# Modulation vectors stored to DRAM after one transpose on TensorE, in rows of 512 bytes

## The chip, the cores and the metric

The kernel runs on one core of one Trainium2 chip. The metric is the device time of an execution in microseconds (us); the median of three runs stands for a kernel.

## The reference

The kernel computes a two-part network on 512 tokens of width 1024. The first part is a block that a condition vector `c` modulates: six vectors of 1024 come from it, and four of them are used late, after the mixer. What matters of it, cut down:

```python
mod_x = silu(c) @ w_mod + b_mod                       # 6 x 1024 values
sh1, sc1, gt1, sh2, sc2, gt2 = split(mod_x, 6)
px = modulate(rms_norm(x, norm1), sh1, sc1) @ w_in    # modulate(h, s, g) = h * (1 + g) + s
...
x = x + gt1 * (concatenate([na_x, hg_x]) @ w_out)
x = x + gt2 * peer_ffn(modulate(rms_norm(x, norm2), sh2, sc2), ...)
```

`na_x` is an attention over neighbours and a context (queries, keys and values are the first 1536 columns of `w_in`), `hg_x` a gated linear recurrence (its forget gates `f` are columns 2048 to 3071). A second part of two layers follows, which the change does not touch.

## The kernel before, in words

Matrix products run on TensorE (PE) with each float32 operand split into a high and a low part, three products for one. A weight tile `w` is loaded by SP into a ring of four (`WBUFS`), ACT writes its high part `wh` and DVE the low part `wl`, two buffers each. Everything is written in the order of generators that `weave` interleaves by their declared costs; each engine then runs its own instructions in order. PSUM has eight banks of 128 x 512, handed out in turn.

The stretch of the change lies in `mixer`. There `weave(self.project_na(first), self.late_mods())` interleaves two things:

- `project_na` projects queries, keys and values. Its last part is the V projection (512 columns in four weight chunks of two k-steps, 18 products each), after which ACT copies four banks into `F`, PE turns them into seven banks of V rows (line 585 and the `ident,F` rows of line 122), and DVE copies two and then seven banks to `V` (lines 577 and 590).
- `late_mods` makes the vectors `gt1`, `sh2`, `sc2` and `gt2`, 1024 values each, held as 128 partitions x 8. Each of the 32 steps (`mod_chunk`) loads 128 rows of `w_mod` transposed (512 KB, through the same ring `w`), multiplies them on DVE by the condition row with a running sum (line 332), and adds the bias (line 333).

The vectors are also needed as rows, the same 1024 values in every partition. `keep_rows` therefore stores each of them (for `sc2` the gain `a2`, line 361) to the DRAM tile `Rd`, through POOL's queue, and `rows_of` later loads a row into all partitions. A vector lies across partitions, so every element of the store is a piece of 4 bytes:

```python
self.nc.gpsimd.dma_start(self.Rd[n].rearrange("(k p) -> p k", p=128), vec)
```

It is called four times, each time as soon as its vector is complete. After that, `lower_bounds` computes a small table `lbm` and stores it to the DRAM tile `Ld` by ACT's queue (line 446, 128 x 2 pieces of 32 bytes). Then `weave(self.project_f(), self.na_tiles(na))` interleaves the projection of the forget gates (`f`, line 611, weights of 256 columns) with 32 tiles of attention: scores (lines 887 and 890), bias added by DVE (892, the bias loaded by SP, 882), maximum (894), exponential on ACT (896), transposes of `P` (903) and products with V.

Of the kernel before, what the change touches and what calls it, by code (L numbers as in the profile page):

```python
# [7 lines left out]
F32 = mybir.dt.float32  # L8
# [4 lines left out]
OP = mybir.AluOpType  # L13
# [3 lines left out]
D = 1024  # L17
S = 512
C = 256
KC = D // 128  # L20
# [31 lines left out]
def run(gen):  # L52
    while True:
        try:
            next(gen)
        except StopIteration as e:
            return e.value


def steps(gen, n):  # L60
    for _ in range(n):
        yield next(gen)


def weave(*gens):

    at = [[0.0, i, g] for i, g in enumerate(gens)]
    while at:
        cur = min(at, key=lambda x: (x[0], x[1]))
        try:  # L70
            cur[0] += next(cur[2])
        except StopIteration:
            at.remove(cur)
# [18 lines left out]
class Net:  # L92
# [262 lines left out]
        self.nc.vector.tensor_tensor(out=m[:, n], in0=b[:, :4].rearrange("p (j i) -> p j i", j=2),  # L355
                                     in1=self.bm[:, n:n + KC + 1:KC].unsqueeze(2).to_broadcast([128, 2, 2]), op=OP.add)

    def gain_of(self, vec, scale, j, name):

        o = self.g.tile([128, KC], F32, name=name)  # L360
        self.nc.vector.scalar_tensor_tensor(o, scale[:, :, j], 1.0, self.gains[:, vec], op0=OP.add, op1=OP.mult)
        return o

    def keep_rows(self, n, vec):

        self.nc.gpsimd.dma_start(self.Rd[n].rearrange("(k p) -> p k", p=128), vec)

    def rows_of(self, n, name, pool):

# [5 lines left out]
    def mixer(self):  # L375
        y = self.pool("y")
        self.Y = y.tile([128, 4, 512], F32, name="Y")
        self.open_stream()
        pj = self.pool("pj")
        hh = pj.tile([128, KC, C + S], FR, name="hh")  # L380
        hl = pj.tile([128, KC, C + S], FR, name="hl")
        self.project_setup(pj, hh, hl)
        first = self.proj(self.p['win'], 0, 512, [self.xs])
        for n in self.mix_norm(hh, hl):
            if n % 2:
                next(first)
        m = self.pool("mixf", "right")
        self.F = m.tile([128, 2, 6, 512], F32, name="F")
        self.mixn = m = self.pool("mixn", "right")
        self.q2 = m.tile([128, 8, S], FR, name="q2")  # L390
        self.k2 = m.tile([128, 8, S + C], FR, name="k2")
        self.ql = m.tile([128, 4, S], FR, name="ql")
        self.V = m.tile([128, 9, 512], F32, name="V")
        weave(self.project_na(first), self.late_mods())
        with self.after(self.last_v):
            self.lower_bounds()
        self.shut("mp")
        na = self.pool("na", "right")
        weave(self.project_f(), self.na_tiles(na))
        self.shut("na")  # L400
        self.shut("mixn")
        m = self.pool("mixi", "right")
        self.I = m.tile([128, 6, 512], F32, name="I")
        self.G = m.tile([128, 4, 512], F32, name="G")
        self.hq = m.tile([128, 4, S], F32, name="hq")
        self.load_bounds()
        q = self.project_q()
        for _ in range(2):
            next(q)
        with self.after(self.last_exp):  # L410
            self.gates()
        run(q)
        self.shut("lbt")
        run(self.project_g())
        hg = self.pool("hg", "right")
        kv = []
        values = self.project_i()
        next(values)
        with self.after(self.log_table(self.last_sig)):
            weave(values, self.hg_keys_decayed(hg, kv))  # L420
        self.shut("pj")
        self.shut("st")
        self.hg_chunks(hg, kv)
# [38 lines left out]
                nc.vector.tensor_tensor(out=f, in0=f, in1=self.lb[:, d:d + 1].to_broadcast([128, 3, 512]), op=OP.add)  # L462

    def late_mods(self):
        self.Rd = self.tc.dram_tile([4, D], F32, name="Rd")
        for j, name in ((2, "gt1"), (3, "sh2"), (4, "sc2"), (5, "gt2")):
            t = self.g.tile([128, KC, 1], F32, name=name)
            setattr(self, name, t)
            for k in range(KC):
                self.mod_chunk(j, t[:, k], k)  # L470
                yield 3.0
            if j in (2, 3, 5):
                self.keep_rows((2, 3, 5).index(j) + (j > 2), t[:, :, 0])
            if j == 4:
                self.a2 = self.gain_of(1, t, 0, "a2")
                self.keep_rows(1, self.a2)

    def mix_norm(self, hh, hl):

# [548 lines left out]
    def peer(self):  # L1028
        nc, p = self.nc, self.p
        hh, hl = self.h2  # L1030
        mv = ([hh[:, k] for k in range(KC)], [hl[:, k] for k in range(KC)])
        first = self.proj_first(self.ws, mv, lambda i: self.normed_half(i, [(hh, hl, self.a2)], 1e-6, self.sh2[:, :, 0]))
        self.finish = None
        for name in ("wo", "st", "hca", "y", "pn"):
            self.shut(name)
        mk = self.pool("mk")
        self.mk = mk.tile([128, 2, 2, C], F32, name="mk")
        self.mv = mk.tile([128, 2, 2, C], F32, name="mv")
        self.open_stream()
        self.Wd = self.tc.dram_tile([TD // WT, 128, 128, WT], F32, name="Wd")  # L1040
        self.Ad = self.tc.dram_tile([AHEAD, 128, TD], F32, name="Ad")
        pg = self.pool("pg", "right")
        self.rows_natural(pg)
        sc = self.queries(mv, first)
        pq = self.pool("pq", "right")
        ac = self.pool("ac")
        pa = self.pool("pa")
        dense = tuple([x[:, T0:] for x in part] for part in mv)
        ahead = self.ahead(pa, dense)
        self.chosen = None  # L1050
        gather = self.gathered(pg, ac)
        with self.tc.manual_schedule(engines={mybir.EngineType.PE}):
            weave(self.route(pq, pg, sc), steps(ahead, AHEAD - REST), self.until_routed(gather))
        self.shut("pq")
        self.shut("psc")
        run(ahead)
        self.shut("pa")
        pm = self.pool("pm", "right")
        ar = self.pool("ar")
        for i in range(GROUP - WLATE):  # L1060
            self.spread_rows(pm, 0, i)
        rows = self.rows_of(3, "gt2r", ar)
        banks = [[self.bank() for _ in range(2)] for _ in range(3)]
        ops = {}
        held = []
        left = self.gather_left
        done = 0
        for e in range(128 + OPS_LAG):
            if e < 128:
                ops[e] = self.operands(pm, e, dense)  # L1070
            want = left * min(e + 1, 120) // 120
            for _ in range(done, want):
                next(gather, None)
            done = max(done, want)
            if e >= OPS_LAG:
                x = e - OPS_LAG
                if x < 128 - TAIL:
                    self.products(banks, range(3), [(x, ops.pop(x))])
                else:
                    held.append((x, ops.pop(x)))  # L1080
        run(gather)
        for t in range(3):
            self.products(banks, [t], held)
        for name in ("pm", "pg", "h2"):
            self.shut(name)
        pt = self.xp = self.pool("pt", "right")
        nf = pt.tile([128, D], F32, name="nf")
        nc.scalar.dma_start(nf, self.rowb(p['normf'], D))
        self.ss = ss = self.sp.tile([128, 4, 2], F32, name="ssx")
        self.xh = {}  # L1090
        self.ws = [self.first_weights(p['awin'], 2304, q) for q in range(2)]
        for t in range(4):
            sq = self.sp.tile([128, 2], F32, name="ssp")
            for h in range(2):
                b = banks[t - 1][h] if t else self.accg[:, h * 512:(h + 1) * 512]
                hs = slice(h * 512, (h + 1) * 512)
                y = pt.tile([128, 512], F32, name="y2", bufs=2)
                nc.vector.tensor_tensor(out=y, in0=b, in1=rows[:, hs], op=OP.mult)
                nc.vector.tensor_tensor(out=self.X[:, t, hs], in0=self.X[:, t, hs], in1=y, op=OP.add)
                self.square_sum(self.X[:, t, hs], sq[:, h:h + 1], pt.tile([128, 512], F32, name="sqx", bufs=2))  # L1100
            r = self.rstd(sq, 1e-6)
            for h in range(2):
                hs = slice(h * 512, (h + 1) * 512)
                nc.vector.scalar_tensor_tensor(self.X[:, t, hs], self.X[:, t, hs], r, nf[:, hs], op0=OP.mult, op1=OP.mult)
                self.square_sum(self.X[:, t, hs], ss[:, t, h:h + 1], pt.tile([128, 512], F32, name="sqx", bufs=2))
            self.unit(t, 1e-5, 4)
        self.shut("ar")
        self.shut("ac")
# [751 lines left out]
```

## Time and profile before

| | |
|---|---|
| median of three runs | 3135.5 us (3133.11 to 3138.17) |
| profiled execution, its time | 3140.31 us |
| profiled execution, its span | 3138.5 us |
| mean granted clock of TensorE | 0.969 of full speed |
| busy: PE, DVE, ACT, POOL | 94%, 60%, 41%, 14% of the span |
| chain that ended last: PE, DVE, DMA | 59%, 18%, 8% of the span |

The profile is of one execution; the times it gives are set against that execution's own time, which is 4.8 us above the median. Busy shares are means over the whole span. What a stretch waits for is read from its own rows: the timeline of an engine gives the idle time before an instruction and what ended it, the table by stretch gives each engine's busy time, the clock that PE was granted (1.00 is full speed), the share of time in which the 16 DMA engines worked, and what they moved.

### The profile page before, as it was taken

What the parts mean: (1) busy time and instruction counts of PE and PEld (TensorE: products, weight loads), DVE (VectorE), ACT (ScalarE), POOL (GpSimd) and SP (SyncE); (2) the same over time, 40 slices, a digit from 0 to 9 for tenths busy, and PEclk for the clock granted to TensorE, in tenths of its full rate; (3) what the DMA queues carried; (4) which work ended last, traced back from release to release, by engine and by line L of the source; (5) the groups of instructions that cost most, each with busy time, mean ns of one, the idle gap of its engine ahead of it and who ended that gap; (6) DMA issues with size and microseconds to landing.
All of it is one profiled execution on the core that took longest, in us unless ns stands there. A gap on an engine that the chain in (4) does not pass through costs nothing.

```text
span 3138.5 us, 42272 instructions
## 1 busy us (share of the span) xinstructions
PE 2946.8 (94%) x16009; PEld 2528.4 (81%) x16009; DVE 1890.9 (60%) x3640; ACT 1271.9 (41%) x2275; POOL 442.8 (14%) x402
## 2 busy tenths in 40 slices
PE   7879898999999999988898888899999999999998
PEld 5668797889899999967677777778888887788887
DVE  5644477639999966678788886544433245543323
ACT  4223464344366677633333323433323234433222
POOL 2200000100211210144454441000000000000000
PEclk9989999999999999999999999999999999999999
DMA  6832202334676776899999996222333222133332
GB/s 244 188 83 72 88 8 68 111 118 135 228 235 220 250 248 238 273 360 372 351 379 370 358 373 220 65 75 89 101 95 100 95 88 68 48 88 100 94 101 81
DMA packets 259148, 539.89 MB, mean 172 GB/s; under 512 B 21632, under 2 KB 136576, under 8 KB 254592
## 3 DMA queue, kind: packets, MB, share of 16 engines
q1 hardware_dynamic: 198368, 347.92, 34.9%
q0 software_dynamic: 36992, 134.25, 11.9%
q10 hardware_dynamic: 23584, 55.03, 4.7%
q8 instruction: 125, 2.05, 0.3%
q14 instruction: 79, 0.65, 0.1%
HBM read 487.02 MB, written 50.09 MB: 171 GB/s over the span
## 4 chain that ended last, share of the span: by engine, by line
PE 59%; DVE 18%; DMA 8%; issue 2%; ACT 1%; SPq 1%; POOL 0%; ACTq 0%; DVEq 0%; POOLq 0%
PE bank L122 57%; DMA act<-Ad 4%; DMA w<-in_V_dram 2%; DVE wl L1351 2%; DVE vl L135 2%; DVE gr L1163 2%; DVE accg L1168 2%; DMA gr<-in_Un_dram,iu 1%; DVE sl L135 1%; PE bank L611 1%; DVE act L1390 1%; PE bank L1499 1%; DVE tmp L1241 1%; DVE eq L1280 1%; DVE eq L1282 1%
## 5 line engine op out<-in xcount | busy, mean ns | idle before, releaser
L122 PE MATMUL bank<-hh,wl 128*128 128x512 f32 (+2 forms) x2304 | 840.5, 365 | 36.3 <-DVE wl L1351 18.4
L122 PE MATMUL bank<-hh,wh 128*128 128x512 f32 (+2 forms) x2304 | 845.4, 368 | 22.6 <-ACT wh L1350 8.8
L122 PE MATMUL bank<-hl,wh 128*128 128x512 f32 (+2 forms) x2304 | 834.4, 362 | 1.4 <-DVE hl L272 0.8
L149 DVE TENSOR_TENSOR wl<-w,wh 128x1024 fp32r<-128x1024 f32 (+2 forms) x280 | 297.1, 1062 | 644.6 <-ACT wh L148 637.6
L148 ACT ACTIVATE wh<-w 128x1024 fp32r<-128x1024 f32 (+2 forms) x280 | 257.4, 920 | 769.3 <-PE bank L122 596.8
L122 PEld LDWEIGHTS bank<-hh,wl 128*128 128x128 f32 x2304 | 439.3, 191 | 95.4 <-DVE wl L1351 26.7
L122 PEld LDWEIGHTS bank<-hh,wh 128*128 128x128 f32 x2304 | 438.7, 191 | 74.8 <-ACT wh L148 9.9
L122 PEld LDWEIGHTS bank<-hl,wh 128*128 128x128 f32 x2304 | 439.3, 191 | 50.8 <-DVE hl L272 1.5
L122 PE MATMUL bank<-vh,sh 128*128 128x512 f32 x768 | 251.5, 410 | 61.8 <-ACT sh L133 61.8
L1144 POOL DMA_INDIRECT gr<-in_Un_dram,iu x128 | 198.8, 1553 | 760.0 <-DVE accg L1168 523.5
L122 PE MATMUL bank<-vh,sl 128*128 128x512 f32 x768 | 245.8, 402 | 1.3 <-DVE sl L135 1.2
L122 PE MATMUL bank<-vl,sh 128*128 128x512 f32 x768 | 246.7, 403 | 0.0
L122 PEld LDWEIGHTS bank<-vh,sh 128*128 128x128 f32 x768 | 149.2, 198 | 102.4 <-ACT sh L133 72.9
L133 ACT ACTIVATE vh<-w 128x1024 fp32r<-128x1024 f32 x128 | 134.6, 1056 | 193.6 <-DMA w<-in_V_dram 169.5
L1351 DVE TENSOR_TENSOR wl<-w,wh 128x1024 fp32r<-128x1024 f32 x128 | 155.8, 1217 | 89.1 <-ACT wh L1350 89.0
L1350 ACT ACTIVATE wh<-w 128x1024 fp32r<-128x1024 f32 x128 | 135.3, 1058 | 153.9 <-PE bank L122 147.1
L122 PEld LDWEIGHTS bank<-vh,sl 128*128 128x128 f32 x768 | 148.6, 195 | 36.8 <-DVE sl L135 5.4
L122 PEld LDWEIGHTS bank<-vl,sh 128*128 128x128 f32 x768 | 149.3, 196 | 35.3 <-DVE vl L135 2.9
L1144 POOL DMA_INDIRECT gr<-in_V_dram,iv x128 | 161.0, 1258 | 83.9 <-DVE accg L1168 37.4
L216 POOL TENSOR_TENSOR r<-r,mhalf 128x1 f32<-128x1 f32 x37 | 21.9, 595 | 1014.1 <-DVE r L215 1007.3
L1168 DVE SCALAR_TENSOR_TENSOR accg<-gr,wt,accg 128x1024 f32<-128x1024 f32 x127 | 162.1, 1276 | 0.1
L135 DVE TENSOR_TENSOR vl<-w,vh 128x1024 fp32r<-128x1024 f32 x128 | 155.6, 1216 | 8.7 <-ACT vh L133 8.7
(367 smaller groups left out, 4719.2 us busy)
## 6 DMA issues: line engine op xcount, KB each, us to landing
w<-in_U_dram SPq DMA_DIRECT2D x128, 512.0 KB
w<-in_V_dram SPq DMA_DIRECT2D x128, 512.0 KB
w<-in_wgu_dram SPq DMA_DIRECT2D x84, 512.0 KB
Wd<-W ACTq DMA_DIRECT2D x24, 1024.0 KB
Wr<-Wd SPq DMA_DIRECT2D x96, 256.0 KB
w<-in_wdown_dram SPq DMA_DIRECT2D x44, 512.0 KB
Ad<-act ACTq DMA_DIRECT2D x116, 192.0 KB
act<-Ad SPq DMA_DIRECT2D x116, 192.0 KB
```

Of the source, the lines that this page charges most:

```text
L122: return self.nc.tensor.matmul(out, a, b, start=start, stop=stop)
L133: self.nc.scalar.activation(hi, src, AF.Copy)
L135: (low or self.nc.vector).tensor_tensor(out=lo, in0=src, in1=hi, op=OP.subtract)
L148: self.nc.scalar.activation(hi[:, :, :n], w[:, :, :n], AF.Copy)
L149: (self.low or self.nc.vector).tensor_tensor(out=lo[:, :, :n], in0=w[:, :, :n], in1=hi[:, :, :n], op=OP.subtract)
L611: nc.tensor.matmul(o, x[k], y[:, kk, :256], start=k == 0 and i == 0 and t % 2 == 0, stop=k == KC - 1 and i == 2, skip_group_check=True)
L1144: nc.gpsimd.indirect_dma_start(out=t, out_offset=None, in_=table, in_offset=bass.IndirectOffsetOnAxis(ap=idx, axis=0))
L1163: nc.vector.scalar_tensor_tensor(t, t, 1.0, self.h0, op0=OP.mult, op1=OP.mult, accum_out=dots[:, h, k:k + 1])
L1168: nc.vector.scalar_tensor_tensor(acc, t, wt[:, h, k:k + 1], acc, op0=OP.mult, op1=OP.add)
L1241: nc.vector.match_replace(tmp, val[:, 0:8], src, -3e38)
L1350: nc.scalar.activation(uh, w, AF.Copy)
L1351: nc.vector.tensor_tensor(out=ul, in0=w, in1=uh, op=OP.subtract)
```

## The change

The four vectors now lie in one tile, `late`, of 128 partitions x 4 x 8. Nothing is stored while they are made. After the woven part, `keep_rows` is called once: PE turns `late` into 32 rows of 128 values in a PSUM bank, ACT copies them to `lr`, and one DMA of POOL's queue stores `lr` to `Rd`, each partition a contiguous piece of 512 bytes. `Rd` holds the same values in the same places as before. The gain `a2` is computed at the end of `late_mods` instead of in `gain_of`.

```diff
--- before.py
+++ after.py
@@ -355,15 +355,14 @@
         self.nc.vector.tensor_tensor(out=m[:, n], in0=b[:, :4].rearrange("p (j i) -> p j i", j=2),
                                      in1=self.bm[:, n:n + KC + 1:KC].unsqueeze(2).to_broadcast([128, 2, 2]), op=OP.add)
 
-    def gain_of(self, vec, scale, j, name):
-
-        o = self.g.tile([128, KC], F32, name=name)
-        self.nc.vector.scalar_tensor_tensor(o, scale[:, :, j], 1.0, self.gains[:, vec], op0=OP.add, op1=OP.mult)
-        return o
-
-    def keep_rows(self, n, vec):
-
-        self.nc.gpsimd.dma_start(self.Rd[n].rearrange("(k p) -> p k", p=128), vec)
+    def keep_rows(self):
+
+        b = self.bank()
+        self.nc.tensor.transpose(b[:32, :128], self.late.rearrange("p n k -> p (n k)"), self.ident)
+        r = self.mp.tile([32, 128], F32, name="lr")
+        self.nc.scalar.copy(r, b[:32, :128])
+        self.Rd = self.tc.dram_tile([4, D], F32, name="Rd")
+        self.nc.gpsimd.dma_start(self.Rd.rearrange("n (k p) -> (n k) p", p=128), r)
 
     def rows_of(self, n, name, pool):
 
@@ -392,6 +391,7 @@
         self.ql = m.tile([128, 4, S], FR, name="ql")
         self.V = m.tile([128, 9, 512], F32, name="V")
         weave(self.project_na(first), self.late_mods())
+        self.keep_rows()
         with self.after(self.last_v):
             self.lower_bounds()
         self.shut("mp")
@@ -462,18 +462,14 @@
                 nc.vector.tensor_tensor(out=f, in0=f, in1=self.lb[:, d:d + 1].to_broadcast([128, 3, 512]), op=OP.add)
 
     def late_mods(self):
-        self.Rd = self.tc.dram_tile([4, D], F32, name="Rd")
-        for j, name in ((2, "gt1"), (3, "sh2"), (4, "sc2"), (5, "gt2")):
-            t = self.g.tile([128, KC, 1], F32, name=name)
-            setattr(self, name, t)
+        self.late = self.g.tile([128, 4, KC], F32, name="late")
+        sc2 = self.g.tile([128, KC, 1], F32, name="sc2")
+        self.gt1, self.a2, self.sh2, self.gt2 = (self.late[:, n] for n in range(4))
+        for j, t in ((2, self.gt1), (3, self.sh2), (4, sc2[:, :, 0]), (5, self.gt2)):
             for k in range(KC):
-                self.mod_chunk(j, t[:, k], k)
+                self.mod_chunk(j, t[:, k:k + 1], k)
                 yield 3.0
-            if j in (2, 3, 5):
-                self.keep_rows((2, 3, 5).index(j) + (j > 2), t[:, :, 0])
-            if j == 4:
-                self.a2 = self.gain_of(1, t, 0, "a2")
-                self.keep_rows(1, self.a2)
+        self.nc.vector.scalar_tensor_tensor(self.a2, sc2[:, :, 0], 1.0, self.gains[:, 1], op0=OP.add, op1=OP.mult)
 
     def mix_norm(self, hh, hl):
 
@@ -1029,7 +1025,7 @@
         nc, p = self.nc, self.p
         hh, hl = self.h2
         mv = ([hh[:, k] for k in range(KC)], [hl[:, k] for k in range(KC)])
-        first = self.proj_first(self.ws, mv, lambda i: self.normed_half(i, [(hh, hl, self.a2)], 1e-6, self.sh2[:, :, 0]))
+        first = self.proj_first(self.ws, mv, lambda i: self.normed_half(i, [(hh, hl, self.a2)], 1e-6, self.sh2))
         self.finish = None
         for name in ("wo", "st", "hca", "y", "pn"):
             self.shut(name)
```

The order of instructions changes at three places. (Line numbers after 371 are four lower in the changed kernel: 611 is 607, 887 is 883, 896 is 892.)

PE, at the end of the V projection, before. The rows `ident,F` are the transposes of V, 611 the f projection, 887 and 890 the scores of the first two attention tiles:

```order
L585 MATMUL bank<-ident,F 128x128 x16
L122 MATMUL bank<-ident,F 64x128 x24
L611 MATMUL bank<-wh,hh 128x256 x3
L887 MATMUL bank<-k_579,q_578 128x256 x2
L890 MATMUL bank<-k_579,ql 128x256 x2
L887 MATMUL bank<-k_579,q_578 128x256 x2
L890 MATMUL bank<-k_579,ql 128x256 x2
L611 MATMUL bank<-wl,hh 128x256
L611 MATMUL bank<-wh,hl 128x256
```

PE, the same place, in the changed kernel:

```order
L581 MATMUL bank<-ident,F 128x128 x16
L122 MATMUL bank<-ident,F 64x128 x24
L361 MATMUL bank<-ident,late 32x128
L607 MATMUL bank<-wh,hh 128x256
L607 MATMUL bank<-wl,hh 128x256
L607 MATMUL bank<-wh,hl 128x256
L607 MATMUL bank<-wh,hh 128x256
L607 MATMUL bank<-wl,hh 128x256
```

And further on, where the first chunk of the f projection ends:

```order
L607 MATMUL bank<-wh,hh 128x256
L607 MATMUL bank<-wl,hh 128x256
L607 MATMUL bank<-wh,hl 128x256
L883 MATMUL bank<-k_579,q_578 128x256 x2
L886 MATMUL bank<-k_579,ql 128x256 x2
L883 MATMUL bank<-k_579,q_578 128x256 x2
L886 MATMUL bank<-k_579,ql 128x256 x2
L607 MATMUL bank<-wh,hh 128x256
```

The transpose of `late` stands between the transposes of V and the f projection, and the first two tiles' scores follow the whole first chunk of the projection (36 products) where they followed three products.

ACT, where the table of lower bounds is made, before (`lbx` is its exponential, `Ld` its store, `wh` a weight chunk's high part):

```order
L440 ACT_TABLE_LOAD
L440 ACTIVATE lbx<-lbx 128x16
L446 DMA Ld<-lbm 128x2x8
L148 ACTIVATE wh<-w 128x2x256 x2
L896 ACTIVATE P,sm<-bank,mx 128x512 x2
L905 COPY PT<-bank 128x512
L896 ACTIVATE P,sm<-bank,mx 128x512 x2
```

ACT, the same place, in the changed kernel:

```order
L440 ACT_TABLE_LOAD
L440 ACTIVATE lbx<-lbx 128x16
L363 COPY lr<-bank 32x128
L446 DMA Ld<-lbm 128x2x8
L148 ACTIVATE wh<-w 128x2x256
L892 ACTIVATE P,sm<-bank,mx 128x512 x3
L148 ACTIVATE wh<-w 128x2x256
L901 COPY PT<-bank 128x512
```

The copy of `lr` stands between the exponential and the issue of the store to `Ld`.

POOL, after the last casts of the queries, before (851 belongs to a much later stage):

```order
L560 TENSOR_TENSOR ql<-F,q_578 64x512
L561 COPY q_578<-q_578 64x512
L366 DMA Rd<-gt_647 128x8x1
L366 DMA Rd<-sh_889 128x8x1
L366 DMA Rd<-a_1252 128x8x1
L366 DMA Rd<-gt_1255 128x8x1
L851 TENSOR_TENSOR r_4111<-r_4111,mhalf 128x2
L851 TENSOR_TENSOR r_4250<-r_4250,mhalf 128x2
```

POOL, the same place, in the changed kernel:

```order
L556 TENSOR_TENSOR ql<-F,q_578 64x512
L557 COPY q_578<-q_578 64x512
L365 DMA Rd<-lr 32x128
L847 TENSOR_TENSOR r_4109<-r_4109,mhalf 128x2
L847 TENSOR_TENSOR r_4248<-r_4248,mhalf 128x2
```

Four stores of 128 x 8 elements became one of 32 x 128. On SP one weight chunk of the f projection moves behind three bias loads that stood after it; the order of DVE's products, copies of V and `wl` up to the end of the modulation is the same.

## Rows read from the trace of the kernel before

**Rows 1.** Timeline of POOL, 92 to 182 us: start us, us, engine, line, operation, tiles.

```profile
92.22 1.16 POOL L366 DMA_DIRECT2D Rd<-gt  x1
120.31 0.91 POOL L366 DMA_DIRECT2D Rd<-sh  x1 [26.93 <-DVE sh L333]
147.49 0.89 POOL L366 DMA_DIRECT2D Rd<-a  x1 [26.27 <-DVE a L361]
173.90 0.89 POOL L366 DMA_DIRECT2D Rd<-gt  x1 [25.53 <-DVE lbm L441]
```

**Rows 2.** Busy time by stretch: engines, then clock, DMA share, GB/s.

```profile
97.00:106.00 9.00, 5.04 (x30) 4.25 (x28) 0.49 (x3) 1.16 (x2) 0.00 (x0) 1.00 0.95 97
106.00:124.00 18.00, 15.64 (x59) 12.31 (x60) 16.56 (x30) 5.36 (x10) 0.91 (x1) 0.81 0.76 250
124.00:135.00 11.00, 11.00 (x51) 9.07 (x49) 0.40 (x3) 0.85 (x1) 0.00 (x0) 1.00 0.97 73
135.00:151.00 16.00, 10.55 (x34) 7.94 (x33) 13.04 (x28) 2.06 (x5) 0.89 (x1) 0.79 0.82 276
151.00:161.00 10.00, 4.83 (x54) 4.17 (x52) 2.19 (x7) 0.50 (x1) 0.00 (x0) 1.00 0.83 79
...
176.00:186.00 10.00, 7.78 (x65) 7.57 (x64) 0.69 (x1) 1.26 (x2) 0.00 (x0) 1.00 0.55 39
```

**Rows 3.** DMA queues, 95 to 105 us: packets, MB, share of 16 engines.

```profile
q1 hardware_dynamic: 467, 1.30, 99.4%
q0 software_dynamic: 32, 0.00, 0.9%
```

**Rows 4.** Who waited for whom, 92 to 200 us: us in total, times, longest.

```profile
DVE mscr L332 <- DMA w<-in_wmt_dram: 32.7, 9, 11.9
```

**Rows 5.** Timeline of PE, 101 to 191 us (in brackets: idle before, and releaser).

```profile
101.68 0.28 PE L122 MATMUL bank<-hh,wl 128*128 128x256 f32 x1
105.92 0.50 PE L122 MATMUL bank<-hh,wh 128*128 128x512 f32 x1 [3.96 <-ACT wh L148]
...
118.88 0.39 PE L122 MATMUL bank<-hh,wh 128*128 128x512 f32 x1
...
122.96 0.39 PE L122 MATMUL bank<-hh,wh 128*128 128x512 f32 x1
...
152.02 1.91 PE L585 MATMUL bank<-ident,F 128*128 128x128 f32 x16
...
165.02 1.97 PE L122 MATMUL bank<-ident,F 128*64 128x128 f32 x16 [9.20 <-DVE V L577]
...
167.93 0.63 PE L887 MATMUL bank<-k,q 128*128 128x256 f32 x2
...
171.69 0.58 PE L611 MATMUL bank<-wl,hh 128*128 128x256 f32 x1 [0.97 <-DVE wl L149]
...
190.41 0.90 PE L903 MATMUL bank<-ident,P 128*128 128x128 f32 x3 [6.63 <-ACT P L896]
```

**Rows 6.** Busy time by stretch, three pieces with their clocks.

```profile
109.20:113.20 4.00, 4.00 (x10) 3.13 (x11) 3.90 (x8) 2.09 (x4) 0.00 (x0) 0.50 0.84 272
190.40:205.70 15.30, 15.29 (x93) 12.58 (x93) 6.11 (x11) 4.29 (x11) 0.00 (x0) 0.51 0.19 53
214.00:234.00 20.00, 20.00 (x208) 17.26 (x202) 9.72 (x18) 6.22 (x14) 0.00 (x0) 1.00 0.24 69
```

**Rows 7.** Timelines of DVE (146 to 175 us) and of ACT.

```profile
147.11 1.22 DVE L332 SCALAR_TENSOR_TENSOR mscr<-w,crow 128x1024 f32<-128x1024 f32 x1
...
148.45 1.22 DVE L332 SCALAR_TENSOR_TENSOR mscr<-w,crow 128x1024 f32<-128x1024 f32 x1
...
165.48 4.26 DVE L590 COPY V<-bank 128x512 f32<-128x512 f32 x7
...
173.47 0.14 DVE L333 TENSOR_TENSOR gt<-gt,bm 128x1 f32<-128x1 f32 x1
...
174.79 0.38 ACTq L446 DMA_DIRECT2D Ld<-lbm  x1
```

## Prediction

> **What bounds the kernel now.** Over the whole span TensorE (PE) is the busy engine, but the change touches only one stretch, so I read that stretch and not the averages. First I looked for the removed stores in the timeline of POOL: four of them, 27 us apart [rows 1]. Then I cut the time around them into pieces and read what the DMA engines moved in each [rows 2]. The reader is to see an alternation. From 2 to 5 us after each store starts, the rate falls from the 250 to 276 GB/s of the pieces between them to 97, 73, 79 and 39 GB/s, for 9 to 11 us, while the DMA share stays at 0.83 to 0.97 in the first three. The engines are not short of work; what they have takes longer. The queue of the stores itself shows nothing of it: 32 packets with 0.9% of the time, while the loads' queue has 99.4% [rows 3]. So the price of the 4-byte pieces, if it is theirs, is paid by the loads beside them.
>
> Who pays is in the waits [rows 4]: the products of the modulation wait 32.7 us for their weight rows. DVE works in order, so what stands behind a product on it (the low halves `wl` of weights, copies of V out of PSUM) is late too, and PE with it. PE's rows [rows 5] give the places: idle for 3.96 us before the V projection, for 9.20 us between the transposes of V (`DVE V`: the copies stood behind products), and for 6.63 us before the first transpose of P. After such gaps the granted clock is 0.50 or 0.51 of full speed, 1.2 instead of 2.4 GHz [rows 6]. From 214 us on PE is busy all the time at clock 1.00 [rows 6]; what comes earlier at that point is carried on.
>
> **What the change removes: three stores during the modulation, and the form of the fourth.** I take three stretches, each from PE's rows, and compare the time it took with the time of its work.
>
> *The V projection*, from the end of the keys at 101.68 + 0.28 = 101.96 to the first transpose of V at 152.02, took 50.06 us [rows 5]. Its work is 4 chunks of 2 k-steps with 18 products each; an undisturbed k-step takes 122.96 - 118.88 = 4.08 us [rows 5], so 8 take 32.7 us. The loss is 17.4 us. Can the loads and DVE keep that pace? From 97 us to the last product that must precede the copies of V, SP has 17 blocks of modulation weights and 2 chunks of V's weights to load, 19 x 0.524 MB = 10.0 MB; at the 250 to 276 GB/s of the pieces between the slow ones [rows 2] that takes 36 to 40 us, to between 133 and 137, where PE would be done at 101.96 + 32.7 = 134.7. So up to 3 us are lost again; I take 2. DVE needs 1.34 us for a product (148.45 - 147.11, [rows 7]); its last 9 follow the fourth chunk's `wl`, which waits for PE's end of the second chunk (101.96 + 16.3 = 118.3), so they end at about 118.3 + 1.2 + 9 x 1.34 = 131.6, before PE. **Term 1: 17.4 - 2 = 15.4 us.**
>
> *The transposes of V and the new wait*, from 152.02 to the row of the f projection at 171.69, took 19.67 us [rows 5]. With DVE ready, its nine copies follow one another at 4.26 / 7 = 0.61 us [rows 7]: 5.5 us. Now comes the price of the change. The new transpose of `late` stands on PE ahead of the f projection and needs the last modulation product. On DVE that product is done 173.47 + 0.14 - (165.48 + 4.26) = 3.9 us after the last copy of V [rows 7], as two products and two `wl` lie between, and their order is kept. PE has nothing to do in that time, as the scores that filled it before now stand behind the projection's first chunk. With 0.3 us for the transpose itself and its start, over twice what one of the 16 transposes at 152.02 takes (1.91 / 16 = 0.12, [rows 5]), the stretch takes 5.5 + 3.9 + 0.3 = 9.7 us. The scores that moved out (from 167.93 to 171.69 - 0.97 = 170.72, 2.8 us at half clock, [rows 5]) cost some 1.4 us later at full clock. **Term 2: 19.67 - 9.7 - 1.4 = 8.6 us.**
>
> *The start of f projection and attention*, from 171.69 to about 214. Lost here are the 6.63 us before P's transpose [rows 5] and half of 15.3 us at clock 0.51 [rows 6], 7.5 us: 14.1 us. The fourth store ends in this stretch, and the slow piece 176 to 186 with it. What stays: after the new wait of 3.9 us PE starts at half clock, for 4 us by the row 109.20 to 113.20 [rows 6], 2 us lost; a start-up of the softmax chain, about 0.5 us; and the store `Ld` that ACT issues at 174.79 [rows 7]. That one has 256 pieces of 32 bytes, a quarter of the pieces of one removed store; at the same price per piece it slows loads for 10 / 4 = 2.5 us, of which I let 1 us reach PE, since four tiles of weights are loaded ahead. **Term 3: 14.1 - 3.5 = 10.6 us.**
>
> *Operations added:* one PE transpose (in term 2); one ACT copy of 32 x 128, between an exponential and the issue of `Ld`, hidden as the next `wh` behind it is for the third chunk of f, two chunks later; were that cover gone it would cost no more than a copy of V on DVE, four times as long a row, 0.61 us [rows 7]. One store of 32 pieces: at the price per piece of the removed ones 10 x 32 / 1024 = 0.3 us of slow loads, at most; nothing if pieces of 512 bytes are not slow. POOL issues one DMA in place of four, of about 1 us each [rows 1], and has nothing else to do then. The new store is issued after the last product, as the fourth one was, and its rows are read first far later, for the output projection of the mixer: nothing waits there. The tile `late` in place of four tiles changes no order on DVE.
>
> Sum: 15.4 + 8.6 + 10.6 = 34.6 us, less 0.6 for the unhidden small things: **34 us**. The profiled execution took 3140.3 us and would take 3106; the median of the runs shown is 4.8 us below it, so I predict 3135.5 - 34 = **3101.5 us**. Bounds: term 1 from 14.4 to 17.4; term 2 from 5 (if the last products wait for loads, not only for DVE) to 10; term 3 from 4 (if `Ld` alone slows the loads as long as the fourth piece shows) to 13. Together 23 to 40.
>
> **The rivals.**
>
> *The stores are innocent by their queue (no difference).* The trace charges them 0.9% of 10 us, about 0.1 us of all engines [rows 3]. If that is their cost, four cost 0.4 us, the slow pieces belong to the loads, and the time stays at 3135 with the new wait hidden. The Trainium skill has a rule of this kind: "DMA: Bandwidth & Descriptors", section Bandwidth, measures a transfer of 4 KB at 0.68 us of DMA time; by it four stores would be worth 2.7 us, under what can be measured here. Rows 2 speak against it: four slow pieces follow four stores, the last among loads of another shape. The same page, Back-pressure in remote DMA, says that stalled writes hold up the other queues of their source engine; it says so of transfers between cores, and rows 2 and 3 look the same here. Chance 4%.
>
> *Slower: the wait of PE for `late`.* If the slow pieces come from the loads themselves, the fourth one and the two before stay, and only the new order remains. Then the first scores, which started at 167.93, stand behind the transpose of `late`, ready at 173.47 + 0.14: 5.7 us later, of which the f projection before them cannot give back anything. With 4 us of half clock after the longer gap, 2 us, it is about 3143 us. It decides if the last product ends more than term 2's gain later than it would without stores, that is if loads are slow anyway. Chance 3%.
>
> *Part of the gain.* `Ld` slows the loads as long as one of the removed stores did (its pieces are short too), the weights in the V projection come at 250 GB/s or less, and PE falls into half clock again between them. Then 12 to 26 us remain, about 20: 3115.5 us. For it speaks that `Ld` is issued within 1 us of the fourth store, so rows cannot part the two; against it that it has a quarter of the pieces. Chance 18%.
>
> **How the numbers follow.** The forecast's case has 75%, with 26 to 40 us of gain: 3095.5 to 3109.5. To leave out no more than 2 in 10 the range takes in the better half of the partial case: 3095 to 3115. A run can tell about 0.2% from no change here, 6.3 us. Both gain cases are above that: faster 0.93; no difference 0.04; slower 0.03.
>
> **What would show it.** In the new profile the rates of 92 to 150 us should stay at 250 GB/s or more until the modulation is done; the products should wait for loads a few us in all and not 32.7; the first transpose of V should start near 137 and the f projection near 147, with an idle gap of about 4 us before the transpose of `late`, released by DVE. One slow piece of 2 to 3 us may follow `Ld`. From there on everything should be as before, some 34 us earlier. I am wrong if slow pieces of 9 us stand where no small store is, if the gap before `late` is 10 us or more, or if the lead at 214 us melts before the end.

## The result and the profile after

The changed kernel takes 3105.6 us (median of four runs, 3099.0 to 3107.7) against 3136.6 us for the kernel before beside it. The ratio is 0.9895, with a 95% interval of 0.988 to 0.991: about 31 us less. The profiled execution took 3107.7 us with a span of 3105.9 us, 32.6 us less than the span before. The forecast was 3101.5 us, with a range of 3095 to 3115.

POOL has one store left in the stretch, where [rows 1] had four:

```profile
150.78 0.78 POOL L365 DMA_DIRECT2D Rd<-lr  x1 [59.09 <-ACT lr L363]
```

Busy time by stretch, changed kernel, to hold against [rows 2] (engines, clock, DMA share, GB/s):

```profile
97.00:106.00 9.00, 7.96 (x42) 6.44 (x41) 6.78 (x15) 5.30 (x10) 0.00 (x0) 1.00 0.83 282
106.00:124.00 18.00, 18.00 (x81) 14.90 (x80) 15.10 (x29) 2.40 (x3) 0.00 (x0) 1.00 0.80 251
124.00:135.00 11.00, 11.00 (x50) 9.11 (x49) 8.29 (x21) 2.35 (x4) 0.00 (x0) 1.00 0.83 301
135.00:144.00 9.00, 5.15 (x66) 4.38 (x64) 7.68 (x16) 1.34 (x3) 0.00 (x0) 0.93 0.76 269
144.00:150.00 6.00, 0.21 (x2) 0.21 (x2) 5.97 (x17) 1.42 (x2) 0.00 (x0) 0.50 0.28 84
150.00:154.00 4.00, 4.00 (x24) 4.00 (x24) 0.39 (x3) 0.25 (x1) 0.78 (x1) 0.64 0.71 208
```

The slow pieces are gone: 97 to 106 us and 124 to 135 us ran at 97 and 73 GB/s before and now run at 282 and 301. The 84 GB/s from 144 to 150 us are no slow piece. The DMA share there is 0.28: the engines had little to do, as the modulation was loaded, and DVE was busy for 5.97 of the 6 us.

Who waited for whom, changed kernel, 92 to 200 us (total, times, longest), with the row that answers to [rows 4] first:

```profile
DVE mscr L332 <- DMA w<-in_wmt_dram: 9.7, 9, 2.4
...
PE bank L361 <- DVE late L333: 7.6, 1, 7.6
...
PE bank L122 <- DVE V L573: 2.1, 1, 2.1
```

The products wait 9.7 us for weights instead of 32.7. The new wait of PE for `late` is there, 7.6 us long. Timeline of PE, changed kernel, at the places of [rows 5]:

```profile
101.10 0.28 PE L122 MATMUL bank<-hh,wl 128*128 128x256 f32 x1
...
135.25 1.91 PE L581 MATMUL bank<-ident,F 128*128 128x128 f32 x16
137.08 1.97 PE L122 MATMUL bank<-ident,F 128*64 128x128 f32 x32
141.15 1.09 PE L122 MATMUL bank<-ident,F 128*64 128x128 f32 x16 [2.10 <-DVE V L573]
149.79 0.40 PE L361 MATMUL bank<-ident,late 128*32 128x128 f32 x1 [7.55 <-DVE late L333]
149.89 0.55 PE L607 MATMUL bank<-wh,hh 128*128 128x256 f32 x1
...
179.89 0.60 PE L899 MATMUL bank<-ident,P 128*128 128x128 f32 x4
```

The last row is the transpose of the sixth tile's P. Before, it stood here:

```profile
213.09 0.60 PE L903 MATMUL bank<-ident,P 128*128 128x128 f32 x4
```

That is 33.2 us earlier. The span is 32.6 us shorter, so nearly all of what is won by 214 us is kept.

### The profile page after: what moved, and what is told of

It reads as the page before. It is cut to its first block, busy times and chain, and to the rows that moved or that the text cites. A ratio compares the mean times of both kernels' runs of the same rounds, so it can differ in the third digit from the quotient of the medians.

```text
span 3105.9 us, 42271 instructions
## 1 busy us (share of the span) xinstructions
PE 2929.4 (94%) x16010; PEld 2511.4 (81%) x16010; DVE 1890.3 (61%) x3640; ACT 1271.7 (41%) x2276; POOL 439.8 (14%) x399
## 4 chain that ended last, share of the span: by engine, by line
PE 57%; DVE 20%; DMA 9%; issue 2%; ACT 1%; POOL 0%; SPq 0%; DVEq 0%; ACTq 0%; POOLq 0%
PE bank L122 55%; DMA act<-Ad 4%; DMA w<-in_V_dram 2%; DVE vl L135 2%; DVE gr L1159 2%; DVE accg L1164 2%; DVE wl L1347 2%; DMA gr<-in_Un_dram,iu 2%; DVE sl L135 1%; DVE act L1386 1%; PE bank L607 1%; PE bank L1495 1%; DVE tmp L1237 1%; DVE eq L1276 1%; DVE eq L1278 1%
```

## The experiments

Theory: four stores of 1024 pieces of 4 bytes slow the loads beside them, and that is what the 31 us were. Rivals: the new order did it, or the loads are slow by themselves. Within the theory it was open what about the stores is dear: the number of pieces, their size, their being neighbours in DRAM, or who writes them. All kernels are edits of the changed one; `Sd` is a spare DRAM tile that nobody reads. The kernel before had medians of 3131.2, 3132.5 and 3131.2 us beside the three groups of runs.

### The stores put back

```diff
         self.late = self.g.tile([128, 4, KC], F32, name="late")
+        self.Sd = self.tc.dram_tile([4, D], F32, name="Sd")
...
                 yield 3.0
+            self.nc.gpsimd.dma_start(self.Sd[j - 2].rearrange("(k p) -> p k", p=128), t)
```

> The changed kernel with the four stores of 4-byte pieces added again, to a spare DRAM tile that nothing reads, each when its vector is complete; every other instruction of every engine stands in the order of the changed kernel. Theory (the stores hold up the loads beside them): four stretches of 9 to 11 us at 40 to 100 GB/s come back after them, the products wait some 33 us for their loads, and the time is 3135 us or a few us more, as the new wait of PE comes on top: 3133 to 3145. Rival (the new order, or one tile in place of four, brought the gain, and the stores are cheap): 3105, four times 0.1 us more.

Measured: 3128.7 us, ratio 0.9986 [0.9975, 0.9998]. Nearly the whole gain is gone, though every other instruction stands in the changed kernel's order. (The time is below the 3133 to 3145 of the theory.) Two stretches, and the wait of the products:

```profile
96.00:105.00 9.00, 7.29 (x42) 6.20 (x40) 0.29 (x2) 0.00 (x0) 0.00 (x0) 1.00 0.50 62
128.00:137.00 9.00, 9.00 (x41) 7.45 (x40) 0.00 (x0) 1.06 (x1) 0.00 (x0) 1.00 0.79 62
```

```profile
DVE mscr L332 <- DMA w<-in_wmt_dram: 32.4, 9, 10.8
```

The first two stores were issued at 91.63 and 123.42 us, and each of these slow stretches follows 4 to 5 us behind. So the stores carry the price, not the order. The rival by which the new wait makes the kernel slower falls here too: it is in this kernel (6.7 us), and the time is still 0.14% below the kernel before.

### What about the pieces is dear

Pieces of 32 bytes, as many and at the same places (`Sd` is `[4, D, 8]`):

```diff
-            self.nc.gpsimd.dma_start(self.Sd[j - 2].rearrange("(k p) -> p k", p=128), t)
+            wide = self.mp.tile([128, KC, 8], F32, name="wide")
+            self.nc.vector.tensor_copy(wide, t.unsqueeze(2).to_broadcast([128, KC, 8]))
+            self.nc.gpsimd.dma_start(self.Sd[j - 2].rearrange("(k p) c -> p k c", p=128), wide)
```

> The changed kernel with four stores added at the same places, of 1024 pieces each as before, but a piece has 32 contiguous bytes (DVE first copies each value eight times, four small copies more; nothing reads the spare tile). If the price goes by the number of pieces: as with 4-byte pieces, 3133 to 3145, and stretches of 9 us at under 100 GB/s. If it goes by what a piece of 4 bytes does in DRAM: the stretches are short, 1 to 3 us, and the time is 3105 to 3113. The store of the lower bounds, 256 pieces of 32 bytes, left no slow stretch in the changed kernel, which speaks for the second.

Measured: 3102.7 us, ratio 0.9909 [0.9892, 0.9927], and the products wait 9.0 us. The time is even below the 3105 to 3113 expected, so 1024 pieces are not dear by their number.

Pieces of 4 bytes, each at the start of its own 512 bytes (`Sd` is `[4, D, 128]`):

```diff
+            self.nc.gpsimd.dma_start(self.Sd[j - 2].rearrange("(k p) c -> p k c", p=128)[:, :, :1], t.unsqueeze(2))
```

> The changed kernel with four stores added at the same places, of 1024 pieces of 4 bytes each, but each piece goes to the start of its own 512 bytes of a spare DRAM tile, so no two pieces are neighbours. If a piece of 4 bytes is dear by itself: 3133 to 3145 and slow stretches of 9 us. If it is dear since neighbours in DRAM come from different partitions and so from different DMA engines, which write into the same few bytes at once: no slow stretch over 3 us, 3105 to 3113.

Measured: 3112.3 us, ratio 0.9934 [0.9917, 0.995]. No slow stretch, and the products wait 9.6 us. A size of 4 bytes does not slow the loads by itself. The time lies within the range expected, but 6.7 us above the changed kernel's 3105.6 and 9.5 above the pieces of 32 bytes; more of that below.

The same with each piece on its own 32 bytes (`Sd` is `[4, D, 8]`), the addresses of the run with pieces of 32:

> As the run with pieces 512 bytes apart (four added stores of 1024 pieces of 4 bytes to a spare tile, beside the late products), but each piece on its own 32 bytes: the addresses of the run with pieces of 32 bytes, and only 4 bytes of each written. Theory (pieces cost because several of them fall into the same few bytes of DRAM; 32 bytes for each is enough, as it was for whole pieces of 32 bytes): no slow stretch, DVE's products wait 9 to 10 us for loads, time 3100 to 3110 us. Rival (a piece of less than 32 bytes costs by itself, unless it lies 512 bytes from the next): slow stretches of some 9 us behind each store, the products wait 25 to 33 us, 3120 to 3130 us.

Measured: 3109.1 us, ratio 0.9933 [0.9913, 0.9952]. The rates stay high and the wait is 11.0 us, so 32 bytes between the pieces are enough:

```profile
96.00:105.00 9.00, 8.10 (x43) 6.46 (x41) 6.12 (x12) 3.21 (x6) 0.00 (x0) 1.00 0.79 277
128.00:137.00 9.00, 9.00 (x45) 7.51 (x44) 7.89 (x19) 2.35 (x4) 0.88 (x1) 1.00 0.92 318
```

Then I asked whether it matters that the neighbours come from different partitions. Here the eight values of 32 bytes come from one:

```diff
+            wide = self.mp.tile([128, KC, 2], F32, name="wide")
+            self.nc.vector.tensor_copy(wide, t.unsqueeze(2).to_broadcast([128, KC, 2]))
+            self.nc.gpsimd.dma_start(self.Sd[j - 2].rearrange("(p k) -> p k", p=128), wide[:, :, 0])
```

> Four added stores of 1024 neighbouring pieces of 4 bytes to a spare tile, beside the late products, but the eight neighbours of each 32 bytes come from one partition (from a copy on DVE in which each value stands apart, four DVE copies of 128x16 added). Theory (the price is that neighbouring pieces come from different partitions, so that several DMA engines write the same few bytes at once): no slow stretch, or a short one, the products wait 9 to 13 us for loads, 3100 to 3112 us. Rival (neighbouring 4-byte pieces cost whoever writes them): slow stretches of some 9 us behind each store, the products wait 25 to 33 us, 3120 to 3130 us.

Measured: 3136.5 us, ratio 1.002 [1.0011, 1.0029]. My theory fell; the time is above the rival's range too (3120 to 3130). The slow stretches are back behind stores at 118.39 and 144.91 us, and the products wait as long as in the kernel before:

```profile
124.00:128.00 4.00, 4.00 (x19) 3.30 (x18) 0.00 (x0) 1.06 (x1) 0.00 (x0) 1.00 1.06 61
149.00:158.00 9.00, 2.94 (x42) 2.53 (x40) 1.17 (x3) 0.00 (x0) 0.00 (x0) 0.86 0.72 48
```

```profile
DVE mscr L332 <- DMA w<-in_wmt_dram: 33.8, 10, 11.3
```

This trace and that of the pieces on their own 32 bytes also give the time from a store's issue to its landing. It is 11.6 to 12.3 us for the four stores here and 5.1 to 6.5 us there. The store issued at 118.39 us landed at about 130.7; from 131 to 145 us the rate is up again (266 GB/s). So the slow stretch lasts until the store has landed.

So 4-byte pieces cost when they lie side by side, and not when each has 32 bytes to itself. That it does not matter which partition writes them rests on the last run, whose values also stand 8 bytes apart in their partition; no run changes that alone. Spacings between 4 and 32 bytes were not run. Nor do the runs tell whether the shared 32 bytes count, or that all 1024 pieces of a store fall into 4 KB of DRAM: with 32 bytes for each they cover 32 KB.

The Trainium skill, "DMA: Bandwidth & Descriptors", section Specifications, puts the smallest transfer for line rate at 512 bytes and says that below this the engine reads, modifies and writes. By size alone that would hold for the pieces of 32 bytes as well, and for those of 4 bytes on their own 32; the waits beside them (9.0 and 11.0 us, 9.7 without stores) show that being under that size does not by itself slow the loads.

### The same stores where nothing is loaded

```diff
         weave(self.hg_states(hg, kv), decays())
+        self.Sd = self.tc.dram_tile([4, D], F32, name="Sd")
+        for n, (d, s) in enumerate(((0, 0), (1, 3), (0, 1), (1, 2))):
+            self.nc.gpsimd.dma_start(self.Sd[n].rearrange("(k p) -> p k", p=128), self.St[:, d, s, :KC])
```

> The changed kernel with four stores of 1024 pieces of 4 bytes added in the recurrence, at about 365 us, where the core's DMA engines move 2 to 27 GB/s (four columns of state tiles go to a spare DRAM tile that nothing reads). Theory (the price is what the loads beside lose): the loads of the output projection's first weights that run there come later, but have some 100 us until they are needed: 3105 to 3109. Rival (a store of this kind holds up the engines that issue or wait, wherever it stands): four times 8 us, 3130 or more.

Measured: 3108.0 us, ratio 0.9923 [0.9906, 0.9939]: no price that can be told from run-to-run differences. The stores ran at 391 to 395 us. Their queue, 390 to 410 us (packets, MB, share of 16 engines):

```profile
q0 software_dynamic: 128, 0.02, 9.5%
```

Four stores took 9.5% of 20 us, so 0.48 us of the 16 engines each. No load moved from 390 to 410 us, so none could be held up; how long these stores took to land, the trace does not say. Beside loads one of them holds up the traffic for 9 us. The Trainium skill, "DMA: Bandwidth & Descriptors", section Bandwidth, gives 0.68 us for a load of 4 KB; the quiet stores are of that order, the 9 us beside loads are not.

### One store of 4096 pieces

```diff
-        b = self.bank()
-        self.nc.tensor.transpose(b[:32, :128], self.late.rearrange("p n k -> p (n k)"), self.ident)
-        r = self.mp.tile([32, 128], F32, name="lr")
-        self.nc.scalar.copy(r, b[:32, :128])
         self.Rd = self.tc.dram_tile([4, D], F32, name="Rd")
-        self.nc.gpsimd.dma_start(self.Rd.rearrange("n (k p) -> (n k) p", p=128), r)
+        self.nc.gpsimd.dma_start(self.Rd.rearrange("n (k p) -> p (n k)", p=128), self.late.rearrange("p n k -> p (n k)"))
```

> No transpose: one store of 4096 pieces of 4 bytes to `Rd` from the four columns of `late`, at the place where the changed kernel has its store of 32 pieces (about 150 us). Theory (each 1024 neighbouring pieces hold the other transfers for 9 to 11 us, whoever waits then): one slow stretch of 36 to 44 us from about 153 to 193 us at 40 to 100 GB/s; the loads that run there (weights of the next stages) land later; what of it reaches the end depends on who needs them, 0 to 30 us, time 3105 to 3135 us. Rival (the price is per store, 10 us each, whatever the pieces): one slow stretch of 10 us, time 3104 to 3112 us.

Measured: 3114.6 us, ratio 0.9946 [0.9931, 0.9961], 13.5 us above the changed kernel on the same chip (3101.1). Three pieces behind the store of 146.63 us, and one wait, 140 to 240 us:

```profile
149.00:152.00 3.00, 3.00 (x27) 3.00 (x26) 0.63 (x1) 0.63 (x1) 0.00 (x0) 1.00 0.85 48
...
158.00:161.00 3.00, 0.00 (x0) 0.00 (x0) 0.00 (x0) 0.00 (x0) 0.00 (x0) 0.70 0.74 40
161.00:164.00 3.00, 0.00 (x0) 0.00 (x0) 0.00 (x0) 0.00 (x0) 0.00 (x0) 0.50 0.55 39
```

```profile
DVE bank L884 <- DMA bias<-in_nab_dram: 13.7, 1, 13.7
```

DVE waits 13.7 us for one bias of 128 KB, issued at 152.55 us, and the attention waits with it. From 152 to 155 us the engines stood nearly idle (DMA share 0.03), as SP asked for the next loads only at 152.09 and 152.55; from 167 us on the rate is up again (164 GB/s). The store landed 16.6 us after its issue, at about 163.2 us. So the slow time is some 16 us: neither the 36 to 44 us of the theory nor the 10 us of the rival, though the time lies in the theory's range. How it grows with the pieces, apart from how much is loaded beside them, these runs do not tell. Putting the four stores into one at the end brings 3132.5 - 3114.6 = 17.9 of the 31.4 us that the changed kernel gains on this chip; the rows of 512 bytes, with the transpose that makes them, bring the rest.

### Can the new wait be had back?

First the changed kernel again, on the chip of the two edits:

> The changed kernel itself, for a median beside the three kernels below on the same chip. Both theories: 3105 us (3099 to 3110), ratio to the kernel before 0.9895; PE's wait for `late` ahead of the transpose at L361 7.5 us, first transpose of P at about 159.5 us.

Measured: 3101.1 us (3099.7 to 3107.2), ratio 0.9905 [0.989, 0.9919]. Then the transpose moved behind the f projection:

```diff
-        r = self.mp.tile([32, 128], F32, name="lr")
+        r = self.g.tile([32, 128], F32, name="lr")
...
-        self.keep_rows()
         with self.after(self.last_v):
...
         weave(self.project_f(), self.na_tiles(na))
+        self.keep_rows()
```

> The transpose of `late` and its store moved behind the f projection and the first attention stretch, so that PE no longer waits for the last late bias ahead of the f projection. Theory (the 7.5 us in which PE waits for `late` are the part of the forecast gain that did not come): f projection and transposes of P begin 6 to 7.5 us earlier than in the changed kernel (first transpose of P at about 152.5 us), the time falls to 3097 to 3101 us. Rival (something else gates the f projection there, the V copies on DVE or the loads of its weights, and the wait only changes its name): PE stands as long at the same place for another releaser, first transpose of P at 157 to 160 us, time 3103 to 3108 us.

And, beside that, `yield 2.5` for `yield 3.0` in `late_mods`:

> As the run with the transpose moved, and the late products are spread over the V projection at a shorter spacing (2.5 us for 3.0 us in the generator), so that DVE is through with them earlier. Theory (DVE's products end at 140.4 us and hold up the copies of V's transposes, which PE waits for): the last products end some 5 us earlier, the V copies start at about 136 us, first transpose of P at 149 to 151 us, time 3094 to 3099 us. Rival (the products are held by the loads of their weights, not by their place in the order): they wait 5 us longer for loads, the V copies start within 1 us of 140 us, and the time is that of the run with the transpose moved.

Measured: 3100.1 us, ratio 0.9902 [0.9886, 0.9917], and 3098.9 us, 0.99 [0.9882, 0.9917]. Neither can be told from the changed kernel. PE with the transpose moved:

```profile
138.82 1.09 PE L122 MATMUL bank<-ident,F 128*64 128x128 f32 x16 [0.78 <-DVE V L573]
140.90 0.62 PE L607 MATMUL bank<-wh,hh 128*128 128x256 f32 x3 [0.99 <-ACT wh L148]
...
145.49 0.58 PE L607 MATMUL bank<-wl,hh 128*128 128x256 f32 x1 [2.42 <-DVE wl L149]
...
174.59 0.60 PE L899 MATMUL bank<-ident,P 128*128 128x128 f32 x4
```

And PE in the changed kernel beside it:

```profile
150.27 0.40 PE L361 MATMUL bank<-ident,late 128*32 128x128 f32 x1 [7.55 <-DVE late L333]
150.38 0.55 PE L607 MATMUL bank<-wh,hh 128*128 128x256 f32 x1
...
180.81 0.60 PE L899 MATMUL bank<-ident,P 128*128 128x128 f32 x4
```

The f projection starts 9.5 us earlier. Of these, 3.0 us came before the edited place: the transposes of V began at 134.23 us instead of 137.27. The `wl` that stands on DVE behind the same products then makes PE wait 2.42 us, and the granted clock is 0.67 over 140 to 150 us. The first transpose of P comes at 158.3 us, 2.1 us earlier than the 160.4 of the changed kernel, where the theory had 152.5 and the rival 157 to 160. With the products spread earlier it comes at 158.6, where 149 to 151 was expected. By that sign the theory fell in both runs, though both times lie in its ranges. At the sixth tile the lead is 6.2 us; the medians show 1.0 us. Later stages vary from execution to execution by nearly as much: the longest one (from the first `sh` to the last `wt` on ACT, at 360 GB/s) took 552 us in the changed kernel's first trace and in that with the transpose moved, and 547 in the changed kernel's second. Where the 5 us went is not settled. With the products spread earlier the copies of V began at 139.60 us and not at 136, as the rival had it, but not for its reason: the products waited less for loads than in the changed kernel (3.4 us, 9.6 there, 92 to 200 us). Instead ACT's `wh` waited 26.2 us for weights of the projections (11.3 there). The loads hold the stretch, whichever of them come first.

### The 6 us of the pieces that lie apart

Their trace had them in the long stage of 360 GB/s: from the first `sh` on ACT at 1283.28 us to the last `wt` at 1838.71 it took 555.4 us, 4 to 8 us more than in the changed kernel's two traces. Was it the place of tensors behind the 2 MB of `Sd`? The tile without the stores:

```diff
         self.nc.gpsimd.dma_start(self.Rd.rearrange("n (k p) -> (n k) p", p=128), r)
+        self.nc.gpsimd.dma_start(self.Sd[0, :32], r)
...
         self.late = self.g.tile([128, 4, KC], F32, name="late")
+        self.Sd = self.tc.dram_tile([4, D, 128], F32, name="Sd")
```

> The changed kernel with the spare DRAM tile of 2 MB of the run with pieces 512 bytes apart, but without that run's four stores: one store of 32 pieces of 512 bytes goes to the tile behind the one to `Rd`. The run with pieces apart stood 6 to 9 us above the changed kernel, and its trace has them between 1300 and 1870 us, where the DMA engines move 360 GB/s without a pause, and nothing of them before. Theory (the place of the tensors that are allotted behind the spare tile makes that stage slower): 3109 to 3114 us, 1300 to 1870 us longer by 6 to 9 us. Rival (the stage varies from run to run, and the four stores or chance made those runs long): 3099 to 3107 us.

> The run with pieces 512 bytes apart once more, beside the one with its spare tile alone. If the place of the tensors behind the spare tile makes the stage from 1300 to 1870 us slower: 3109 to 3114 us here too, and the same beside it. If chance did: 3099 to 3107 us here. No slow stretch before 200 us by either.

Measured: 3102.9 us for the tile alone, ratio 0.9913 [0.99, 0.9927], and 3108.7 us with the stores again, 0.9928 [0.9914, 0.9942]. The place of the tensors is not it; the second time lies just under the range for that and above the range for chance. The long stage took 550.1 us in the second trace with the stores, so the 555.4 did not come back. The three runs with pieces apart stand at 3108.7 to 3112.3 us, and the four stores where nothing is loaded at 3108.0, while the runs without such pieces stand at 3101.1 to 3105.6. So a price of some 6 us for four stores of 4-byte pieces stays possible, wherever they stand; but the intervals of all four overlap that of the tile alone, and the traces have no place for it. That stays open.

## Why the prediction was right, step by step

**The mechanism** held. The loads beside the stores pay, as the sum assumed, and removing the 4-byte neighbours removes all four slow pieces. That the stores might be innocent by the 0.9% of [rows 3] was refuted by putting them back.

**Term 1, the V projection: foretold 15.4 us, measured 16.2.** From the end of the keys (101.10 + 0.28) to the first transpose of V (135.25) it takes 33.87 us instead of 50.06. PE's products run without a gap but one of 1.04 us.

**Term 2, the transposes of V and the new wait: foretold 8.6 us, measured 3.6.** This is the one step of the sum that failed: it came out below its own bound of 5. From 135.25 to 149.89 us the stretch takes 14.64 us, where the sum had 9.7. Timeline of DVE, changed kernel:

```profile
137.16 1.22 DVE L332 SCALAR_TENSOR_TENSOR mscr<-w,crow 128x1024 f32<-128x1024 f32 x1 [0.65 <-DMA w<-in_wmt_dram]
...
139.14 1.23 DVE L332 SCALAR_TENSOR_TENSOR mscr<-w,crow 128x1024 f32<-128x1024 f32 x1 [0.55 <-DMA w<-in_wmt_dram]
...
140.40 1.29 DVE L573 COPY V<-bank 128x512 f32<-128x512 f32 x2
141.61 4.27 DVE L586 COPY V<-bank 128x512 f32<-128x512 f32 x7
...
149.59 0.15 DVE L333 TENSOR_TENSOR late<-late,bm 128x1 f32<-128x1 f32 x1
```

The two durations in the sum were right: the nine copies take 141.61 + 4.27 - 140.40 = 5.48 us (5.5), and `late` follows them by 149.59 + 0.15 - 145.88 = 3.86 us (3.9). What was missing lies ahead of the copies: 5.15 us from 135.25 to 140.40. Of these, 1.91 us are the first 16 transposes, which the copies need and the sum left out. The other 3.24 us are the last products, expected to end at 131.6 by DVE's pace and between 133 and 137 by the loads', and done at 140.40. The fourth chunk's `wl`, put at 118.3 in the sum, began at 122.88. I had counted 10.0 MB of loads, 17 blocks of modulation weights and 2 chunks of V's. From 97 to 140.4 us SP issued 19 blocks, 3 chunks of V's and 2 of f's, and the engines moved 12.3 MB, at 284 GB/s: the ring of four lets SP load ahead of what the copies wait for. The bound of 5 was meant for such loads; the 1.91 us take the term below it.

**Term 3, the start of f projection and attention: foretold 10.6 us, measured 12.8.** From the f projection's row at 171.69 [rows 5] to the sixth tile's transpose, 171.69 to 213.09 became 149.89 to 179.89: 41.40 to 30.00 us, 11.4 less, with the first scores (1.4 us, charged to term 2) moved into it. The clock is back at 1.00 by 154 us. `Ld` is issued at 150.49 us and no slow piece follows: no price shows for its 32-byte pieces, as in the run with pieces of 32. I had left 3.5 us for it and for the start, 0.5 of them for the softmax chain without a row behind it, and no run parts that out; the rival that lets `Ld` hold back part of the gain fell on that ground.

Together 16.2 + 3.6 + 12.8, and 0.6 us by which the keys ended earlier, are the 33.2 us of lead. Against the 34 foretold, the 5.0 us that term 2 lost are nearly made up by 0.8 and 2.2 from terms 1 and 3, by the keys' 0.6, and by the 0.6 set aside for small things, of which nothing shows. That the total came so near is in part luck, as these errors happened to offset each other. Of the 33.2 us, 32.6 are left in the span and 31.0 in the medians.

**The wait for `late`** was expected at about 4 us and is 7.55: seven copies of V run on for 3.64 us after PE's last transposes of V (141.15 + 1.09 to 145.88), and the 3.86 us come on top. Taking it away gave nothing that a measurement shows, so the transpose's place is not worth an edit here.

## What to carry to other kernels

A store whose pieces are single 4-byte values next to each other in DRAM was paid here by the loads beside it: look at the rate of the other queues a few us after it, not at its own share. Turning the tile on PE, so that each partition stores a contiguous row, removed that; so did pieces of 32 bytes for each value, and, but for some 6 us that stay open, 4 bytes in their own 32, or storing where nothing is loaded. When a wait is removed, count what stands on the next engine in line, every instruction and every load, up to the one that will be waited for: here the copies of V, held by the loads, missed their time.

## What the runs showed that was not expected

One store of 1024 neighbouring pieces of 4 bytes takes 0.48 us of the DMA engines when they are idle, and holds loads at 40 to 100 GB/s for about 9 us when they are not, until it has landed (11.6 to 12.3 us after its issue, in the one run of this kind that has that time). The same number of pieces costs the loads beside it nothing that shows with 32 bytes to each (waits of 9.0 to 11.0 us, 9.7 without stores), whether all 32 are written or only 4. Neighbours from one partition cost as much as neighbours from eight (33.8 and 32.4 us of waiting). What in the chip does this no run shows.
